# An encoder layer on eight cores: smaller bias table, reordered loads and stores, work moved between VectorE, GpSimd and ScalarE

**Chip, cores, metric.** One Trainium2 chip, all 8 cores, each with its own share of the tokens. The metric is the device time of the slowest core in microseconds (us). A program on all cores has a second, slower state in some of its executions: the four cores of one die, or of both, show a lower granted TensorE clock (0.82 to 0.96 in the slow runs of the changed kernel, 0.98 in its fast ones) and the run takes longer (4537 to 5164 us instead of 4422 to 4430). "Fast" below means a run without that. Four runs of the kernel before were there at the start, with a median of 4583.62 us (4518.32 to 4875.31); two of the four were fast.

## The reference, cut to what matters

```python
h = rmsnorm(x); q, k, v, u = split(h @ w_in)       # D = 2048, 16 heads of 64, 1024 pooling channels
attn = longnet(q, k, v)     # three dilated windows (128,1), (512,4), (2048,16), ALiBi penalty
pool = per group of 256 channels: mean over 2/4/8/16 tokens minus the token, a linear map, a scale
x = x + concat(attn, pool) @ w_out
x = x + relu(rmsnorm(x) @ w1) ** 2 @ w2            # DFF = 8192
y = rmsnorm_final(x)
```

## The kernel before

A scheduler records every operation with the tiles it reads and writes and derives the waits. Each core goes through these stages: K and V of ten half blocks of 512 tokens; the pooling channels of three units of 1024 tokens, with Q; attention in 24 steps; then for each of three units the output projection and the FFN. K, V, h and the attention result go through HBM. "SP" is the queue that issues plain transfers; weights, f32 in HBM and bf16 in their tiles, come through GpSimd's queue (the FFN's in loads of 2048 KB, a median of 14.9 us each in the kernel before). An evacuation is the copy of a finished group of matmuls out of PSUM, where TensorE leaves it (L419: 128x512 in a median of 681 ns). A run is a stretch of contiguous bytes in HBM that a transfer reads. A queue stands while it waits for a semaphore before it can issue its next transfer (from 421 to 452 us SP's stood 16.27 and 13.33 us). `acts` is the result of attention and pooling, x the input of the layer, X the residual that the output projection adds to.

The four places the argument touches, cut (cuts marked `# ...`):

```python
def prep(i):                       # half i of x becomes hT (scaled) and c0 (sum of squares)
    for q in range(4):             # x comes in four quarters of 1 MB
        # ... 4 scalings on VectorE (L366); Square on ScalarE
        if q > 0:
            S.pool(... c0.ap = c0.ap + b.ap ...)          # 2048 wide, L376
            if i + 1 < NHS: load_x(4 * i + q + 4)
    # ... two halving adds on VectorE (L384, L386)

# in first_k(i), i < 2:
for _ in prep(i + 1): pass         # the whole preparation of the next half ...
if i == 0: load_wv()
for m in (6, 7): k_group_mms(...); k_evac(i, m, b)        # ... ahead of two K evacuations (L419)

# in the V loop of half i, group gi:
win0 = window_copy("L0", 6, (0, 5), 2)                    # HBM to HBM, 2 copies of 2 MB
if i == 5 and gi % 4 == 2: next(win0)

# last attention step, and the FFN's first weights:
if si == NSTEP - 1 and it == 0:
    load_acts(UORD[0])             # both halves of the attention result, runs of 1 KB
    load_wo(0)
    for q in range(4): load_res(UORD[0], 0, q)            # residual X
# ... load_wo(1), load_wo(2), load_wo(3) straight behind
for m in range(16):
    oproj(1, m)
    # ...
    if m == 3: load_w1(0)          # 2 MB
```

The softmax here doesn't subtract the row's maximum and nothing guards it: scores larger than these inputs give would overflow.

## Time and profile before

Stages are read from the first and last start of four kinds of instruction on every core: the V evacuations, the exponentials of attention, the relus of the FFN and the last operation on y. The mean of the eight cores of the profiled (fast) run:

| stage | from, to | us |
|---|---|---|
| start | 0 to first V evacuation | 197.2 |
| K/V loop | to last V evacuation | 471.6 |
| pooling and Q | to first exponential | 222.0 |
| attention | to last exponential | 476.8 |
| entry to the FFN | to first relu | 160.3 |
| FFN, with two changes of unit | to last relu | 2881.2 |
| end | to last operation on y | 92.3 |
| sum | | 4501.4 |

Spans of the cores run from 4487.7 to 4524.1 us. The lines behind each stage stand in the prediction; in a timeline line the bracket at the end is the idle time before the group and what ended it.

### The profile page before, as it was taken

The numbers are of one execution on the slowest core, as the hardware profiler recorded it, in microseconds if no ns is written. First come the engines' busy times: TensorE is split into PE (matmuls) and PEld (weight loads), VectorE is DVE, ScalarE is ACT, GpSimd is POOL, SyncE is SP. The second block draws the span as 40 slices with busy tenths as digits, with TensorE's granted clock in tenths as the row PEclk, the third lists the DMA queues.
The fourth block names the chain that finished last, engine by engine and source line by source line (L and its number), as shares of the span: only waits on it lengthen the run. The fifth ranks groups of instructions, "written<-read, shape, count | busy, mean of one in ns | idle before, by whom it ended". The sixth has DMA issues, their size and how long they took to land.

```text
span 4524.1 us, 62014 instructions; the slowest of 8 cores (4487.7 to 4524.1 us)
## 1 busy us (share of the span) xinstructions
PE 4265.9 (94%) x23228; PEld 2085.8 (46%) x23228; DVE 2248.8 (50%) x3383; ACT 905.0 (20%) x1218; POOL 507.2 (11%) x381
## 2 busy tenths in 40 slices
PE   6799999799995999999999899999999899999996
PEld 2344445377773444444444344444444344444442
DVE  2224427866661344455556344444446445444446
ACT  1122210087782100000002100000002100000002
POOL 2122212300001200000005200000004200000003
PEclk8899999899998999999999999999999899999998
DMA  7376758499997533333355623333345623333332
GB/s 177 107 208 175 212 127 198 121 254 255 247 250 192 93 75 75 75 75 75 75 112 148 149 60 79 80 80 77 75 85 148 158 57 75 77 80 79 79 77 75
DMA packets 187077, 556.11 MB, mean 123 GB/s; under 512 B 14658, under 2 KB 118210, under 8 KB 158402
## 3 DMA queue, kind: packets, MB, share of 16 engines
q0 software_dynamic: 19536, 249.05, 28.2%
q1 hardware_dynamic: 167250, 303.09, 23.4%
q8 instruction: 194, 3.18, 0.3%
q14 instruction: 97, 0.79, 0.1%
HBM read 715.13 MB, written 105.91 MB: 181 GB/s over the span
## 4 chain that ended last, share of the span: by engine, by line
PE 80%; DMA 8%; DVE 5%; POOL 2%; issue 2%; SPq 1%; another core or an unknown queue 1%; ACT 1%; DVEq 0%; POOLq 0%; ACTq 0%
PE ps L296 80%; DMA y<-arena 3%; POOL arena L1048 1%; DVE arena L643 1%; SPq L140 1%; DMA arena<-wk 1%; POOL arena L376 1%; DVE arena L657 1%; DVE arena L1062 1%; DMA VD<-VD 1%; DVE arena L366 1%; DMA arena<-HT 1%; DMA arena<-xkv 1%; DMA arena<-xres 0%
## 5 line engine op out<-in xcount | busy, mean ns | idle before, releaser
L296 PE MATMUL ps<-arena 128*128 128x512 bf16 (+4 forms) x23228 | 4265.9, 347 | 238.0 <-DMA arena<-ACTD 42.9
L296 PEld LDWEIGHTS ps<-arena 128*128 128x128 bf16 x23228 | 2085.8, 102 | 2416.5 <-issue 319.0
L1097 DVE TENSOR_TENSOR arena<-ps,arena 128x512 f32<-128x512 f32 x1536 | 1052.6, 691 | 241.7 <-PE ps L296 239.7
L1087 DVE TENSOR_TENSOR arena<-arena 128x512 bf16<-128x512 f32 x384 | 265.3, 692 | 1056.9 <-ACT arena L1086 1056.9
L1086 ACT ACTIVATE arena<-ps 128x512 f32<-128x512 f32 x384 | 229.3, 597 | 2255.7 <-PE ps L296 2255.7
L140 POOL DMA_DIRECT2D arena<-w x96 | 51.0, 534 | 2362.1 <-PE ps L296 2361.3
L881 ACT ACTIVATE arena<-ps 128x1024 bf16<-128x1024 f32 x288 | 282.4, 1020 | 106.8 <-PE ps L296 87.2
L1048 POOL TENSOR_TENSOR arena<-arena 128x512 f32<-128x512 f32 x180 | 239.2, 1329 | 361.3 <-ACT arena L1047 348.5
L897 DVE TENSOR_TENSOR arena<-arena 128x1024 bf16<-128x1024 bf16 (+2 forms) x384 | 205.4, 556 | 94.4 <-ACT arena L881 86.7
L1073 DVE TENSOR_TENSOR arena<-ps,arena 128x512 f32<-128x512 f32 x96 | 65.6, 686 | 264.6 <-DMA arena<-xres 153.1
L1047 ACT ACTIVATE arena<-arena 128x512 f32<-128x512 f32 x180 | 113.2, 630 | 337.7 <-DVE arena L1073 276.6
L366 DVE TENSOR_SCALAR arena<-arena 128x512 bf16<-128x512 f32 x160 | 113.3, 762 | 132.0 <-DMA arena<-xkv 111.8
L376 POOL TENSOR_TENSOR arena<-arena 128x2048 f32<-128x2048 f32 x27 | 123.2, 4561 | 464.7 <-ACT arena L371 464.1
L419 DVE TENSOR_TENSOR arena<-ps,arena 128x512 bf16<-128x512 f32 x80 | 53.2, 684 | 103.4 <-PE ps L296 98.3
L447 ACT ACTIVATE arena<-ps,arena 128x512 bf16<-128x512 f32 x80 | 53.5, 687 | 252.2 <-PE ps L296 121.0
L371 ACT ACTIVATE arena<-arena 128x2048 f32<-128x2048 f32 x40 | 75.7, 1906 | 138.4 <-DVE arena L366 138.2
L944 DVE TENSOR_TENSOR arena<-ps,arena 64x512 bf16<-64x512 f32 x96 | 62.0, 684 | 77.2 <-ACT arena L938 77.2
L1062 DVE SCALAR_TENSOR_TENSOR arena<-arena 128x512 f32<-128x512 f32 x96 | 90.7, 987 | 3.4 <-ACT arena L325 3.4
L1057 DVE SCALAR_TENSOR_TENSOR arena<-arena 128x512 bf16<-128x512 f32 x96 | 74.1, 816 | 4.8 <-ACT arena L325 4.8
L631 POOL TENSOR_TENSOR arena<-arena 128x1039 f32<-128x1039 f32 x24 | 60.0, 2500 | 135.3 <-DVE arena L795 117.9
L140 POOL DMA_DIRECT2D arena<-wo x12 | 6.4, 539 | 581.1 <-PE ps L296 581.1
L322 DVE TENSOR_SCALAR arena<-ps 128x512 f32<-128x512 f32 (+1 forms) x23 | 15.3, 667 | 112.5 <-PE ps L296 112.5
(38 smaller groups left out, 471.3 us busy)
## 6 DMA issues: line engine op xcount, KB each, us to landing
arena<-w POOLq DMA_DIRECT2D x96, 2048.0 KB, 14.9
arena<-xkv SPq DMA_DIRECT2D x40, 1024.0 KB, 7.9
arena<-VD SPq DMA_DIRECT2D x72, 512.0 KB, 9.7
VD<-arena SPq DMA_DIRECT2D x48, 512.0 KB, 8.7
arena<-wo POOLq DMA_DIRECT2D x12, 2048.0 KB, 23.5
arena<-xres SPq DMA_DIRECT2D x24, 1024.0 KB, 7.1
y<-arena SPq DMA_DIRECT2D x96, 256.0 KB, 6.6
arena<-KT SPq DMA_DIRECT2D x144, 128.0 KB, 4.0
```

Of the source, the lines that this page charges most:

```text
L140: return self.op(eng, lambda e: e.dma_start(out=out() if callable(out) else out, in_=in_() if callable(in_) else in_), reads, writes, key=key)
L296: S.pe(lambda e: e.matmul(out, lhsT=lhsT, rhs=rhs, start=start, stop=stop, skip_group_check=skip), reads, writes)
L366: S.dve(lambda e, b=b, k=k, kc=kc: e.tensor_scalar(out=t[:, kc, :], in0=b[:, k, :], scalar1=cst[:, G1 + kc:G1 + kc + 1], scalar2=None, op0 ...
L376: S.pool(lambda e, b=b: e.tensor_tensor(out=c0.ap, in0=c0.ap, in1=b.ap, op=ALU.add), [c0.r(), b.r()], [c0.r()])
L881: S.act(lambda e: e.activation(out=e_.ap, in_=ps[:, 512 * sb:512 * sb + 1024], func=AF.Exp, scale=0.125), [P(sb), P(sb + 1)], [e_.r()])
L897: S.dve(lambda e, ov=ov, iv=iv, tv=tv: e.tensor_tensor(out=ov, in0=iv, in1=tv, op=ALU.mult), [e_.r((c0, c0 + n)), tb.r(hl)], [p_.r((c0, c0 ...
L1047: S.act(lambda e: e.activation(out=s_.ap, in_=x[:, m, :], func=AF.Square), [x.r(m)], [s_.r()])
L1048: S.pool(lambda e: e.tensor_tensor(out=acc[h].ap, in0=acc[h].ap, in1=s_.ap, op=ALU.add), [acc[h].r(), s_.r()], [acc[h].r(), ("serial",)])
L1062: S.dve(lambda e: e.scalar_tensor_tensor(out=X[h][:, m, :], in0=X[h][:, m, :], scalar=cst[:, GF + m:GF + m + 1], in1=rb3[h].ap, op0=ALU.mu ...
L1086: S.act(lambda e: e.activation(out=r_.ap, in_=ps8[:, b, :], func=AF.Relu), [P(b)], [r_.r()])
L1087: S.dve(lambda e: e.tensor_tensor(out=a_[:, fc, 512 * h:512 * h + 512], in0=r_.ap, in1=r_.ap, op=ALU.mult), [r_.r()], [a_.r(fc, (512 * h, ...
L1097: S.dve(lambda e: e.tensor_tensor(out=X[h][:, m, :], in0=ps8[:, b, :], in1=X[h][:, m, :], op=ALU.add), [P(b), X[h].r(m)], [X[h].r(m)])
```

## The change

Its intent is to close the places where TensorE waits: at the start, at the window copy, in the pooling stage, at the entry to the FFN, and at each change of unit; and to shrink the bias table so that one multiply does the work of two. Cut to its core:

```diff
-TABW = 1280
+TABW = 768                                   # one 256-wide table per pattern; masked blocks by strided PSUM columns
-y  [3, 2, 16, 128, 512]   ACTD [3, 2, 16, 128, 512]
+y  [3, 2, 128, 16, 512]   ACTD [3, 2, 128, 16, 512]      # 16 KB runs; y stored in pairs
 # prep: halving adds 1024, 512, 512, on GpSimd for q < 3, on VectorE for q = 3
+            op = S.pool if q < 3 else S.dve
 # first_k: only half of the next preparation ahead of the evacuations
-            for _ in prep(i + 1): pass
+        for _ in range(4): next(gn, None)
         if i == 0: load_wv()
         for m in (6, 7): ...
+        for _ in gn: pass
 # window copy: four copies of 1 MB in halves 4 to 7
-    win0 = window_copy("L0", 6, (0, 5), 2)
+    win0 = window_copy("L0", 6, (0, 5), 4)
-            if i == 5 and gi % 4 == 2:
+            if 4 <= i <= 7 and gi == 2:
 # pooling: the first add moves from GpSimd to VectorE, with a multiply; PSUM evacuation to ScalarE
-        S.pool(... s1 = uu + uu shifted ...)
+        S.dve(... uu = uu * rb ...)
+        S.dve(... s1 = uu + uu shifted ...)
 # entry to the FFN
+            if si == 18 and it == 2: load_acts(UORD[0], 0)
             if si == NSTEP - 1 and it == 0:
-                load_acts(UORD[0])
                 load_wo(0)
+                load_acts(UORD[0], 1)
 # ... load_wo(1..3) wait for X; the first evacuations lag by up to five groups
 # change of unit
-            pop_tail(2)
+            pop_tail(4 if m < 3 else 2)           # stores of y leave earlier
 # ... residual loads are asked for behind later stores
```

## The prediction

> **What bounds the kernel now.** I read the cores first: spans of 4487.7 to 4524.1 us, the two dies within 0.1%, so the profiled run is undisturbed. The four timed runs are 4518.32, 4519.07, 4648.17 and 4875.31 us; the last two are the slow state, and I predict against 4518.7, the fast pair. Then the table by stretches, which shows what a busy stage looks like:
>
> ```profile
> 1695.00:1808.00 113.00, 113.00 (x525) 51.18 (x524) 55.29 (x81) 10.16 (x17) 2.11 (x4) 1.00 0.36 75
> 904.00:1017.00 113.00, 111.76 (x1399) 87.90 (x1397) 75.67 (x129) 92.35 (x99) 0.00 (x0) 1.00 1.01 255
> ```
>
> The first is the FFN: TensorE has no gap, 525 matmuls in 113 us. In the long FFN stretch 3962 matmuls take 858 us, 0.2166 us each. It is over half of the span and the diff does not touch it. The second is attention: TensorE again has no real gap, but DMA is at 1.01, so nothing may be added there. What can be won lies where TensorE waits; I listed its timeline and kept the lines with a gap in brackets:
>
> ```profile
> 87.26 31.05 PE L296 MATMUL ps<-arena 128*128 128x512 bf16 x133 [20.20 <-DVE arena L419]
> 124.50 2.29 PE L296 MATMUL ps<-arena 128*128 128x512 bf16 x5 [6.19 <-DVE arena L366]
> 146.80 28.52 PE L296 MATMUL ps<-arena 128*128 128x512 bf16 x120 [20.01 <-DVE arena L419]
> 1417.79 22.42 PE L296 MATMUL ps<-arena 128*128 128x512 bf16 x90 [42.86 <-DMA arena<-ACTD]
> 2554.70 0.59 PE L296 MATMUL ps<-arena 128*128 128x512 bf16 x1 [11.10 <-DVE arena L1057]
> ```
>
> Two gaps of 20 us at the start wait for the K evacuation (L419); one of 43 us waits for the attention result read back from HBM; one of 11 us is at a change of unit. What holds L419 back stands in the timelines of GpSimd and VectorE:
>
> ```profile
> 69.61 14.37 POOL L376 TENSOR_TENSOR arena<-arena 128x2048 f32<-128x2048 f32 x3 [63.63 <-ACT arena L371]
> ...
> 84.49 1.22 DVE L384 TENSOR_TENSOR arena<-arena 128x1024 f32<-128x1024 f32 x1 [14.15 <-POOL arena L376]
> 85.82 0.69 DVE L386 TENSOR_TENSOR arena<-arena 128x512 f32<-128x512 f32 x1
> 86.43 1.28 DVE L419 TENSOR_TENSOR arena<-ps,arena 128x512 bf16<-128x512 f32 x2
> ```
>
> [...] the sum of squares of the next half waits 14 us for three GpSimd adds of 4.5 us, and the two evacuations that free PSUM banks stand behind it. The pooling stage (695 to 897 us) is bound by VectorE:
>
> ```profile
> 706.70 5.43 DVE L643 TENSOR_TENSOR arena<-arena 128x1037 f32<-128x1037 f32 x3
> ...
> 743.35 1.70 DVE L651 TENSOR_TENSOR arena<-arena 128x16 f32<-128x16 f32 x1
> ...
> 764.12 3.86 DVE L657 SCALAR_TENSOR_TENSOR arena<-arena 128x256 bf16<-128x256 f32 x4 [0.18 <-DVE arena L651]
> ```
>
> Three adds should be 3 x 1.23, a 16-element multiply is 0.17 elsewhere, four L657 are 2.14 elsewhere. Each chunk has one operation that is about 1.6 us too long, while GpSimd runs L631. Last, the change of unit, as the chain of work has it:
>
> ```profile
> 2505.13 41.42 DMA y<-arena
> 2546.78 6.33 DMA arena<-xres
> ```
>
> The last residual load waits for four output stores that took 41 us, against 6.5 for the group before them; VectorE stood 24.12 us for that load and TensorE 11 behind it.
>
> [...] L643 is 1.23 or 2.76 us, and L366 between 0.47 and 4.75. [...] a 2 MB weight load was issued from GpSimd at 2502.94, the four stores at 2503.14. [...] Here the first six matmuls after the gap of 42.86 took 2.72 us, 0.45 each.
>
> **The change, part by part.**
>
> *Start.* The sum of squares is cut into halving adds (1024, 512, 512 wide), GpSimd takes three quarters and VectorE the fourth, and the two evacuations now stand after the first eight of sixteen scalings instead of after the whole preparation. The evacuations then run at 67 instead of 86.4, so the first gap falls from 20.2 to under 1. GpSimd's chain is as long as before (estimate 13 to 14 us, from 1.3 us per 512 and 1.9 to 2.3 per 1024), but starts one quarter earlier and nothing but the sum waits on it. The second gap goes likewise, but there the next 1 MB of x (13.3 us to land in this trace) becomes the limit: it is asked for near 90 instead of 110.5, while 4 MB of Wv, which moved to about 77, and three x quarters are in flight. At the 180 GB/s of 90 to 120 us in this trace, 8 MB from 77 are through by 118 (estimate), so I let it land at 113 instead of 123.9. That is 10 us on that wait plus 19 of the second gap. Sum: 29 us at 146.8, not 40.
>
> *Window copy.* Two copies of 2 MB in one half become four of 1 MB in four halves. Before, the queue stood 16.27 + 13.33 us at 421 to 452, x came late and 52 matmuls, 11 us, were missing in 452 to 565. I give it 8, as each small copy still waits for the last V store.
>
> *Pooling stage.* The add L631 moves from GpSimd to VectorE, the PSUM evacuation (2 x 0.75) to ScalarE (2 x 0.6, idle there), and VectorE gets one 1024-wide multiply. Per chunk on VectorE: minus 1.51, minus about 1.6 of blocking, plus 1.23 and 1.24: minus 0.6. Per unit of eight chunks the old rates are 2 x (9.52 + 8.2 + 6.85 + 6.2) = 61.5; new 2 x (8.97 + 7.74 + 6.5 + 5.28) = 57.0, against TensorE's 8 x 6.93 = 55.4. Three units: 13.5; I take 12, since the 8.2 us wait for an ACTD store stays.
>
> *Attention.* Two multiplies (556 + 285 ns) become one (692): 96 x 0.149 = 14 us of VectorE, which is 67% busy there and not on the path: 0. The table falls from 640 to 384 KB, 6% of a step's estimated 4.3 MB; the gaps near the loads of HT (about 15 us in all over two places) shrink a little, but a 2 MB load of acts enters at step 18 of 24. The matmuls have the same number and width, with strided PSUM columns. Net 2.
>
> *Into the FFN.* The first half of acts is loaded five steps early, in 16 KB runs instead of 1 KB; the second half, the first weights and X follow in the last step, later weights behind X, and the first evacuations lag five banks. TensorE can start near 1376, if the first weight tile (issued at 1355.5, 15 us alone, sharing with 6 MB) has landed. About 18 MB remain to be moved; at 300 to 380 GB/s, which the large packets reached from 1418 to 1448, that ends near 1420 to 1430, about as TensorE consumes them. I take 37 of 42.9, with 6 left as small stalls.
>
> *Change of unit, twice.* Stores become 512 KB pairs, residual loads are asked for after later stores, so the queue need not stand, and the tail is popped twice as fast in the first three steps, so all stores are out before the FFN weights come. From the matmul counts the first change loses 31 us ((1048 - 904) x 0.2166, from 2373 to 2600), the second 36. What stays: 6.46 us for the GpSimd square chain before the first row norm, about 2 for the second norm, which is now asked for earlier than GpSimd finishes, and about 2.5 of restart. So 20 + 25 = 45.
>
> *End.* Same chain, last store twice as big: 0 to minus 1.
>
> Sum: 29 + 8 + 12 + 2 + 37 + 45 = 133; 4518.7 - 133 is 4386; I say 4390.
>
> **The rivals.** First, DMA takes the place of the waits removed: the start and the entry to the FFN were both at a DMA share of 1.0 while TensorE stood (1.00 from 1376 to 1418). If bytes are all that counts, they give 10 and 20 instead of 29 and 37, and the time is 4426. For it: the share. Against: 165 to 177 GB/s there, against 384 later at the same share[...]. Second, attention pays: with a share of 1.01 the early acts load or strided PSUM writes stop a step; 1% of slower matmuls costs 5 us, a doubled HT gap 10: 4400. Third, VectorE becomes the bound in preparation, blocked by nine short GpSimd adds instead of three long ones, and K evacuations come late in all ten halves: 1 to 2 us each, 4405. Fourth, all gaps close: 20 + 20 + 43 + 60 + 12 + 11 = 166, 4353.
>
> **Range and chances.** The first two together make about 4435, the fourth 4353. Eight times in ten the time lies in 4350 to 4455; the upper end also holds a median that a slow run has touched. Two per cent is 90 us: it needs a third of my sum to fail. Faster by over 2%: 0.87; within: 0.12; slower: 0.01.
>
> **What will show it.** Gaps before the matmuls near 68 and 114 us: under 1, and about 17. No VectorE wait of 14 us for GpSimd at 84. No L643, L651 or L657 beyond 1.3, 0.2 and 0.6 us each, and the pooling stage some 190 instead of 202 us. Attention steps at 19.2 us. The first matmul of the output projection within 7 us of attention's last. VectorE's waits for xres (153.1 us in all before) mostly gone, and no y store of 40 us; the 6.46 us gaps stay. I am wrong if the attention step grows, if the weights of the output projection arrive one by one after TensorE wants them, or if K evacuations wait for the new adds.

## The result, and the profile after

The changed kernel took a median of 4483.37 us over 10 runs (4422.13 to 5163.88), the kernel before 4594.09 over 15 runs beside it (4516.2 to 5119.31). Half of the 10 runs were slow, and so were 8 of the 15. The five fast runs lie between 4422.13 and 4430.09, the seven fast ones of before between 4516.2 and 4523.0. Ratios here are the mean time of one kernel's fast runs over that of the other's fast runs of the same rounds, so not quite the ratio of the medians: 0.9793, 95% interval 0.978 to 0.9806. The fast time fell by 94 us; the prediction had 129.

By stage, mean of eight cores, with the prediction's term beside it:

| stage | before | after | gained | predicted |
|---|---|---|---|---|
| start | 197.2 | 177.0 | 20.2 | 29 |
| K/V loop | 471.6 | 469.6 | 2.0 | 8 |
| pooling and Q | 222.0 | 216.5 | 5.5 | 12 |
| attention and entry | 637.1 | 605.5 | 31.6 | 2 + 37 |
| FFN, two changes of unit | 2881.2 | 2846.9 | 34.3 | 45 |
| end | 92.3 | 92.1 | 0.2 | 0 |
| sum | 4501.4 | 4407.6 | 93.8 | 133 |

Every term but the last came out smaller. The predicted terms were read on core 5, the slowest of the kernel before. From there to core 2, the slowest of the changed kernel, the gains are 19.3, 2.1, 7.6, 27.4, 42.9 and 0.4, in all 99.7: the changes of unit are nearly as predicted on that core. Taken apart, attention went from 476.8 to 475.8 and the entry from 160.3 to 129.8. TensorE's timeline of the changed kernel, its groups behind a gap of interest:

```profile
67.47 19.80 PE L296 MATMUL ps<-arena 128*128 128x512 bf16 x89 [0.87 <-DVE arena L416]
...
124.00 1.91 PE L296 MATMUL ps<-arena 128*128 128x512 bf16 x4 [26.97 <-DVE arena L366]
...
613.55 230.00 PE L296 MATMUL ps<-arena 128*128 128x512 bf16 x1219 [8.78 <-ACT arena L444]
...
1347.69 15.01 PE L296 MATMUL ps<-arena 128*128 128x512 bf16 x62 [1.65 <-DMA arena<-wo]
1375.16 104.00 PE L296 MATMUL ps<-arena 128*128 128x512 bf16 x457 [12.46 <-DMA arena<-wo]
...
2489.32 872.59 PE L296 MATMUL ps<-arena 128*128 128x512 bf16 x3958 [0.71 <-DVE arena L1057]
```

The first 20 us gap is down to 0.87, the 43 us gap at the entry to 1.65 and 12.46, the 11 us gap at the change of unit to 0.71. But the second gap at the start grew from 20 to 27, and there is a new one of 8.78 us at 613. The chain of work names what these two waited for:

```profile
89.22 33.66 DMA arena<-xkv
...
580.69 31.94 DMA VD<-arena
```

A quarter of x (1 MB) took 34 us to land, where it had taken 13 in the kernel before; a V store (512 KB) took 32. Both times weights had been issued from GpSimd's queue shortly before (at 580.07 the second time, 0.6 us ahead of the store), here at the start:

```profile
76.38 4.47 POOL L140 DMA_DIRECT2D arena<-wv x8
```

And VectorE's timeline, at the K evacuation (L416) and in the pooling stage:

```profile
66.64 1.28 DVE L416 TENSOR_TENSOR arena<-ps,arena 128x512 bf16<-128x512 f32 x2
...
696.65 3.91 DVE L645 TENSOR_TENSOR arena<-arena 128x1037 f32<-128x1037 f32 x3
...
731.09 2.12 DVE L659 SCALAR_TENSOR_TENSOR arena<-arena 128x256 bf16<-128x256 f32 x4 [9.02 <-DMA ACTD<-arena]
...
746.23 1.23 DVE L631 TENSOR_TENSOR arena<-arena 128x1024 f32<-128x1024 f32 x1 [1.97 <-ACT arena L797]
```

The evacuations run at 66.64 as predicted. The three adds that took 5.43 us take 3.91. New are waits of 1.97 us for ScalarE's evacuation, three on each core. The wait for a store of the pooling result is 9.02 us here and 9.3 to 14.2 on the other cores (mean 11.5); before it was 7.9 to 10.1 (mean 8.9).

In attention and at the entry the columns of the table by stretches are: stretch, its length, busy time and count of PE, PEld, DVE, ACT and POOL, granted clock, DMA share, GB/s:

```profile
904.00:1017.00 113.00, 110.65 (x1376) 87.89 (x1399) 74.47 (x106) 92.64 (x99) 0.00 (x0) 1.00 0.94 247
...
1350.00:1375.00 25.00, 12.64 (x58) 5.49 (x56) 0.00 (x0) 0.00 (x0) 1.59 (x3) 0.84 1.03 230
```

The DMA share is near 1 from 900 to 1400 (0.92 to 1.02 in stretches of 100 us on core 2), while TensorE is busy and while it waits.

### The profile page after: what moved, and what is told of

It reads as the page before. It is cut to its first block, busy times and chain, and to the rows that moved or that the text cites.

```text
span 4424.4 us, 61370 instructions; the slowest of 8 cores (4403.6 to 4424.4 us)
## 1 busy us (share of the span) xinstructions
PE 4226.2 (96%) x22791; PEld 2081.9 (47%) x23228; DVE 2252.3 (51%) x3296; ACT 938.6 (21%) x1266; POOL 450.7 (10%) x402
## 3 DMA queue, kind: packets, MB, share of 16 engines
q1 hardware_dynamic: 148850, 296.79, 23.3%
## 4 chain that ended last, share of the span: by engine, by line
PE 78%; DMA 8%; DVE 6%; POOL 3%; SPq 2%; issue 2%; ACT 1%; DVEq 0%; POOLq 0%; ACTq 0%
PE ps L296 78%; SPq L140 2%; DMA VD<-arena 2%; POOL arena L1048 2%; DMA arena<-xkv 2%; DVE arena L366 1%; DMA arena<-wk 1%; DMA VD<-VD 1%; DMA arena<-wo 1%; DVE arena L659 1%; DVE arena L645 1%; DVE arena L1062 1%; DVE arena L633 1%; DVE arena L631 1%; DVE arena L416 0%
## 5 line engine op out<-in xcount | busy, mean ns | idle before, releaser
L896 DVE TENSOR_TENSOR arena<-arena 128x1024 bf16<-128x1024 bf16 x288 | 198.8, 692 | 99.5 <-ACT arena L885 98.3
L366 DVE TENSOR_SCALAR arena<-arena 128x512 bf16<-128x512 f32 x160 | 127.6, 851 | 150.6 <-DMA arena<-xkv 130.5
L416 DVE TENSOR_TENSOR arena<-ps,arena 128x512 bf16<-128x512 f32 x80 | 53.3, 685 | 111.6 <-PE ps L296 106.6
L374 POOL TENSOR_TENSOR arena<-arena 128x1024 f32<-128x1024 f32 x27 | 64.2, 2379 | 429.8 <-ACT arena L402 255.5
L659 DVE SCALAR_TENSOR_TENSOR arena<-arena 128x256 bf16<-128x256 f32 x96 | 51.3, 604 | 13.1 <-DMA ACTD<-arena 9.0
## 6 DMA issues: line engine op xcount, KB each, us to landing
arena<-w POOLq DMA_DIRECT2D x96, 2048.0 KB, 13.8
```

The source lines that it names most:

```text
L366: S.dve(lambda e, b=b, k=k, kc=kc: e.tensor_scalar(out=t[:, kc, :], in0=b[:, k, :], scalar1=cst[:, G1 + kc:G1 + kc + 1], scalar2=None, op0 ...
L659: S.dve(lambda e, i0=i0, i1=i1, oo=oo: e.scalar_tensor_tensor(out=oo, in0=i0, scalar=1.0 / w, in1=i1, op0=ALU.mult, op1=ALU.subtract), [cu ...
L896: S.dve(lambda e: e.tensor_tensor(out=p_.ap.rearrange("p (a b) -> p a b", b=256), in0=e_.ap.rearrange("p (a b) -> p a b", b=256), in1=tv, ...
```

## The experiments

Eighteen kernels ran, all with the right result; seventeen are edits of the changed kernel and one (e6) of the kernel before. Unless said otherwise a figure is the mean of the eight cores of a fast profiled run, and each edit of the changed kernel is compared with the 177.0, 469.6, 216.5 and 605.5 us of the table. Each is one profiled run, and the cores of one run differ: in the changed kernel four cores have 464 us in the K/V loop and four 473 to 478, and pooling is 214 or 219. The runs differ as well. In the undisturbed profiles whose edit leaves a stage alone, its mean is 174.1 to 177.0 us at the start, 464.3 to 469.6 in the K/V loop, 215.2 to 219.2 in pooling and 601.9 to 605.6 in attention and entry. The changed kernel's own profile stands at the upper end of three of these, so a gain measured from it can be up to 5 us too large, and a loss as much too small; differences under 5 us need a wait in the trace to back them.

### The start: weights of V beside x

**e1**: the loads of Wv moved behind the requests for x, by making them wait for a tile of x.

```diff
-... wv_d[:, 2 * k:2 * k + 2, :], [],
+... wv_d[:, 2 * k:2 * k + 2, :], [xs[0].r()],      # and issued in the next half
```

> The changed kernel, but the eight Wv loads wait until the first quarter of x for the third half has landed. Theory: that quarter, asked for at 89 us, took 34 us to land only because it shares the DMA engines with Wv. Then it lands in 10 to 15 us, the gap of 27 us before the third half's matmuls at 124 falls to 7 to 12, Wv still lands before the first V matmul, and attention starts 15 to 20 us earlier (its first exponential at about 850 instead of 867). Rival 1, bytes are all that counts: the gap falls, but the first V half then waits for Wv, and attention starts at 862 to 868. Rival 2, the quarter is behind the three other quarters of x in its own queue: it still takes over 25 us and nothing moves.

The quarter of x landed near 101 and the gap of 27 us fell to 5.59. But the start stayed at 177.2: a new gap of 22.75 stood at 149. The loads of Wv had become readers of the x buffer, and its next writer, ScalarE's square, waited for them. That is an artifact of the edit; the total settles nothing, the gap does. **e1b** takes a wait without that side effect, on the first scaled column of the third half.

```diff
-... wv_d[:, 2 * k:2 * k + 2, :], [],
+... wv_d[:, 2 * k:2 * k + 2, :], [hT[2].r(0)],      # and issued in the next half, as in e1
```

> The first try at holding Wv back made the squares of the third half wait for Wv as well, because the loads were marked as readers of the x buffer that the squares overwrite; that closed nothing. Here the Wv loads wait for the first scaled column of the third half instead, which nothing overwrites soon. Theory: the first quarter of x lands in 10 to 15 us as in that run, the gap of 27 us falls to under 8, the third half's sum of squares is not late any more, and the first V evacuation comes at 155 to 165 us instead of 177. Rival: Wv (30 us of transfer from about 101) now is what the first V half waits for, and the first V evacuation comes at 170 or later.

The quarter of x landed in 12.6 us, the start took 153.7 us, 23.3 less, and the run 4400.07. TensorE's timeline, and GpSimd's:

```profile
101.54 2.29 PE L296 MATMUL ps<-arena 128*128 128x512 bf16 x5 [5.52 <-DVE arena L366]
```

```profile
101.94 4.99 POOL L140 DMA_DIRECT2D arena<-wv x8 [17.85 <-DVE arena L366]
```

With Wv issued at 102 instead of 76 the gap is 5.5 us. The change moved the evacuations off the path as planned; that it gained 20 us and not 43 is the collision of x with Wv (the quarter took 33.66 us to land beside Wv, 12.6 ahead of it).

### The K/V loop

**e3**: the weights for folding the pooling map (wuT, 4 loads) wait for the last V store of half 8.

```diff
-... wuT_d[:, 2 * k:2 * k + 2, :], [],
+... wuT_d[:, 2 * k:2 * k + 2, :], [("VD", HS[8][0], 4 * HS[8][1] + 3)],
```

> The changed kernel, but the four wuT loads (1 MB each) wait until the last V store of the ninth half (i=8) has landed. Theory: the stall of 8.8 us of TensorE at 613 us, which the kernel before does not have, comes from wuT being issued 0.6 us before four V stores that then take 32 us to land. Then the stores land in under 15 us, the stall is under 1 us, no new wait for wuT appears at the weight product near 640, and attention starts 7 to 10 us earlier. Rival: the stores come late because their mask fill on VectorE stands behind the preparation of the next half; then the stall stays over 5 us.

Two of its three runs were slow, and in the profiled one cores 2 and 3 ran at clock 0.973. On the six other cores the K/V loop took 464 to 466 us. Time from issue to landing of the V stores at 570 to 600 us, core 2 of the changed kernel:

```profile
DMA to landing us min/median/max: 31.8/31.9/32.1
```

Core 4 of e3, and its TensorE, which has no gap where core 2 had 8.78:

```profile
DMA to landing us min/median/max: 3.3/4.2/5.3
```

```profile
539.68 140.58 PE L296 MATMUL ps<-arena 128*128 128x512 bf16 x827
```

So the slow stores come from wuT beside them: a V store takes 26.7 us or more on every core of the changed kernel, and at most 9.1 on the six cores of e3. But the stores stop TensorE on three cores of the changed kernel only (0, 2 and 6, by 8.3, 8.8 and 11.1 us), and in e4b (below), which leaves this part as it is, on none. The gain is that of some cores. The pooling stage took 220.3, 3.8 more; 2.3 of that is a longer wait for the pooling store, and that mean is near the scatter, so no cost of the later weights is shown.

**e11** put the bias table back to its old size, the extra 256 KB a step loaded but unused. It was meant for attention (below), and showed something else too.

```diff
-TABW = 768
+TABW = 1280           # the columns beyond 768 stay zero
```

> The changed kernel with only the bias table back at its old size (640 KB a step instead of 384, the extra 256 KB unused). The sum of the two stages from the first to the last attention exp and from there to the first relu was 605.5 us (mean of 8 cores) in the changed kernel and 637.1 in the kernel before. Theory A (these stages are set by what the DMA engines have to move; share 0.98 to 1.04 from 900 to 1400): 24 x 256 KB is 6.3 MB, at some 250 GB/s 25 us, so the sum grows by 15 to 25 us. Theory B (my prediction: TensorE sets the attention step, the table hardly matters): plus 0 to 5.

The K/V loop rose from 469.6 to 490.8 on all cores: the table is cast from HBM to HBM in this loop, 640 KB a half instead of 384. SP's queue and VectorE show how 256 KB cost that much. SP:

```profile
336.62 0.75 SPq L140 DMA_DIRECT2D VD<-arena x1
353.06 0.68 SPq L140 DMA_DIRECT2D VD<-VD x1
```

VectorE:

```profile
495.44 0.88 DVE L366 TENSOR_SCALAR arena<-arena 128x512 bf16<-128x512 f32 x2 [24.55 <-DMA arena<-xkv]
```

The queue stands 15.7 us between a V store and the window copy, because the copy waits for the V store just issued; x, asked for behind it, comes late. In the changed kernel the same stand is there (460.83 to 475.64), but x comes just in time: four cores have 464 us. **e15** keeps the old table and puts the copy ahead of this half's V stores:

```diff
-            if 4 <= i <= 7 and gi == 2:
+            if 4 <= i <= 7 and gi == 0:      # with TABW = 1280
```

> The changed kernel with the old table size (as e11) and the four small window copies put behind the first V group of a half instead of the third, so before this half's V stores instead of just behind one. With the old table the K/V loop took 488 to 494 us on the 8 cores; TensorE alone needs 464. Theory A (the queue stands 15 us for the V stores ahead of each copy, x is asked for late, and the larger table then makes it late enough to stop TensorE): the queue's stand before each copy falls under 3 us and the K/V loop to 464 to 474. Theory B (the bytes of the larger table as such): 485 or more.

```profile
338.18 4.55 SPq L140 DMA_DIRECT2D HT<-arena x1
343.24 0.98 SPq L140 DMA_DIRECT2D VD<-VD x1
```

The stand is 0.5 us, and the K/V loop 474.2, just above the range of theory A: three cores at 464, and five at 478 to 481, which are the cores with the wuT stall (8.9 to 12.6 us at 612 to 617). So the standing queue made 16.7 of the 21 us. Splitting the window copy hid it in the changed kernel because the smaller table made room.

### Pooling

**e9** puts the first add back on GpSimd.

```diff
-        S.dve(lambda e: e.tensor_tensor(out=s1[:, 1:1040], ...
+        S.pool(lambda e: e.tensor_tensor(out=s1[:, 1:1040], ...
```

> The changed kernel with the first pooling add back on GpSimd. Theory A ([...] each such add stretches one VectorE operation by about 1.6 us, more than the 1.23 that VectorE saves): one of L643/L651/L653/L659 per chunk beyond its usual length again, the pooling stage of 216.5 us (mean of 8 cores) plus 3 to 10. Theory B (the blocked VectorE time wasn't what bound the stage): within 2 or shorter.

Its runs were slow; in the profiled one cores 4 to 7 were, and on the undisturbed die (cores 0 to 3) pooling took 222.3, 219.7, 223.9 and 221.1 us against 213.6 to 214.4 there in the changed kernel, 7.8 more in the mean. The size is less sure than the sign: the same four cores have 214.0 to 220.6 in twelve runs that leave pooling alone, and 2.1 of the 7.8 are a longer wait for the store. Chunk by chunk on core 2 e9 takes 0.1 to 0.4 us longer, about 5 us in 24 chunks. GpSimd, then VectorE:

```profile
694.24 2.79 POOL L633 TENSOR_TENSOR arena<-arena 128x1039 f32<-128x1039 f32 x1 [6.22 <-DVE arena L631]
```

```profile
694.00 5.45 DVE L645 TENSOR_TENSOR arena<-arena 128x1037 f32<-128x1037 f32 x3
```

Three adds take 5.45 us beside the GpSimd add and 3.91 without: 1.54 us lost, as the prediction read it; VectorE gets most of that back, as it has the add no longer.

**e2** lets the pooling buffers go round by a running count of chunks instead of the chunk number modulo 3, which reuses a buffer too soon where a unit changes.

```diff
-        uu = ub[m % 3]
+        uu = ub[cidx(u, m) % 3]        # cidx = 8 * u + 7 - m; the same for ap_
```

> The changed kernel, with the three pooling buffers taken in turn by a chunk counter instead of by m modulo 3 (the same for the three output tiles). Theory: at the two changes of unit the old numbering gives m=7 the buffer of m=1, two chunks back, so that ScalarE's evacuation starts only when VectorE is done, and VectorE then waits 1.97 us for it, four times; with the counter these waits of VectorE for ScalarE go, and the pooling stage (first ScalarE evacuation to first attention exponential, 193 us) is 4 to 8 us shorter. Rival: the stage is bound elsewhere (TensorE at 6.93 us a chunk, or the 9 us wait for an ACTD store), and the stage shrinks by less than 2.

The waits of 1.97 us are gone (three on each core, not the four that were expected), and the stage is 213.3, 3.2 less, between the theory and its rival. The wait for the store stays (14.0 us on core 2, 7.5 on core 5), and six cores have a second one of 2.2 to 3.4 us. The run, 4431.13, shows nothing of it, since cores 2 and 3 ran at clock 0.978. **e10** makes the other two window copies, which pass in this stage, one transfer each instead of two.

```diff
-window_copy("L2", 8, (0, 2), 2)      window_copy("R1", 7, (3, 5), 2)
+window_copy("L2", 8, (0, 2), 1)      window_copy("R1", 7, (3, 5), 1)
```

> The changed kernel, with each of the two window copies of the pooling stage made as one DMA of 4 MB instead of two of 2 MB, of which the second waits for the first in the queue with the stores of the pooled tiles behind it. Theory: VectorE's wait of 9 to 14 us for an ACTD store at about 722 to 731 us falls to under 3 us, and the pooling stage (last V evacuation to first exponential, 217 us in the mean over the cores) is 6 to 10 us shorter. Rival: the store is slow because the copy fills the DMA engines; then the wait stays over 6 us.

215.1 us, and the wait for the store 4.6 to 13.8, over 6 on six of the cores: the rival, and within the scatter.

### Attention and the entry to the FFN

Back to **e11**: attention and entry rose from 605.5 to 617.1, 11.6 us for the table alone; theory A had 15 to 25, the prediction next to nothing. e15, with the same old table, has 616.3. Three runs undo one part of the entry each. **e12** takes the old layout of the attention result (1 KB runs), **e13** loads its first half in the last step and not at step 18, **e5** frees the second weight load from waiting for X.

```diff
 # e12
-ACTD [3, 2, 128, 16, 512]
+ACTD [3, 2, 16, 128, 512]
 # e13
-            if si == 18 and it == 2: load_acts(UORD[0], 0)
+                load_acts(UORD[0], 0)          # in the last step, with the other half
 # e5
-                load_wo(1, [X[0].r((0, 4))])
+                load_wo(1)
```

> The changed kernel with only the layout of the attention result in HBM as before (runs of 1 KB instead of 16 KB in the three 2 x 2 MB reads). Theory A (DMA time of small runs is what the entry to the FFN had lost; the prediction put most of its 37 us on it): the sum of attention and entry, 605.5, grows by 8 us or more, and the two loads take over 25 us each. Theory B (only the order of the loads and the lag of the evacuations matter): plus 0 to 4.

> The changed kernel with the first half of the attention result loaded with the second in the last attention step, not at step 18. Theory A (the stages from 900 to 1400 are bound by the DMA engines as a whole, so it doesn't matter where the 2 MB are moved): the sum 605.5 stays within 4 us, attention gets 8 to 10 shorter, the entry that much longer. Theory B (the early load is what hides the entry, as predicted): attention 3 to 6 shorter, the entry over 12 longer, sum plus 8 or more.

> The changed kernel, but the second weight tile of the output projection does not wait for the first quarter of X. Theory: it is issued at about 1331 instead of 1352.5 and lands 10 us or more before the 1375 of the changed kernel; the gap of 12.5 us falls to under 5, the time from the last attention exponential to the first relu falls from 125 to 136 us by 6 to 10. Rival: DMA is at its limit from 1326 to 1406 whatever the order; then the first weight tile, the evacuations or the later tiles come late by as much, and that time stays within 3 us.

The sums are 605.3, 604.5 and 604.6: nothing, three times. In e13 attention is 10.3 shorter and the entry 9.2 longer, as theory A had it. In e5 four cores have 484 to 491 us in attention and 117.5 in the entry, the other four 466 to 472 and 132 to 137: the wait moves, the sum stays. Taken alone, this would say that the layout and the early load are worth nothing. They replace each other, as **e16** and **e17** show. e16 takes the order of the kernel before, with 16 KB runs; e17 that order with 1 KB runs.

```diff
 # e16
-            if si == 18 and it == 2: load_acts(UORD[0], 0)
-                load_wo(0)
-                load_acts(UORD[0], 1)
+                load_acts(UORD[0], 0)
+                load_acts(UORD[0], 1)
+                load_wo(0)                     # load_wo(1..3) without waiting for X
 # e17: the same, and ACTD as in e12
```

> The changed kernel (small table, 16 KB runs, lagged evacuations) with the loads of the entry to the FFN in the order of the kernel before: both halves of the attention result first and in the last step, then the first weights and X; no weight load waits for X. Attention plus entry was 605.5 (mean of 8 cores). Theory A (order: four weight loads of 2 MB side by side with the result and X delay what TensorE needs first): plus 10 to 20. Theory B (all bytes must pass anyway): within 4.

> As e16 and the attention result in runs of 1 KB as before; what then still differs from the entry of the kernel before are the table and the lag of the evacuations. Theory A (order and layout make the remaining 20 us together): 620 to 628. Theory B (order alone): as e16 within 3. Theory C (the lag): under 612.

e17 has 625.8 us, and the old gap is back. TensorE, then SP's queue:

```profile
1377.56 116.51 PE L296 MATMUL ps<-arena 128*128 128x512 bf16 x518 [42.02 <-DMA arena<-ACTD]
```

```profile
1317.58 49.32 SPq L140 DMA_DIRECT2D arena<-ACTD x2
1367.04 12.06 SPq L140 DMA_DIRECT2D arena<-xres x4
```

e16 has 597.2, better than the changed kernel by 8, which neither theory had. TensorE, then SP's queue:

```profile
1347.82 29.77 PE L296 MATMUL ps<-arena 128*128 128x512 bf16 x125 [8.12 <-DMA arena<-ACTD]
1383.47 88.56 PE L296 MATMUL ps<-arena 128*128 128x512 bf16 x393 [5.88 <-DVE arena L1079]
```

```profile
1322.73 0.92 SPq L140 DMA_DIRECT2D arena<-ACTD x2
```

Issuing the two loads took 49.32 us in 1 KB runs (48.8 of them for the second) and 0.92 in 16 KB runs, and they landed after a median of 62.5 us against 33.7, beside the same weight loads. X could be asked for only at 1367. The books close: from 637.1 to e17's 625.8 is 11.3 (table and lag of the evacuations; e11 gave 11.6 for the table), from there to e16's 597.2 is 28.6 (layout, in the old order), and the new order gives 8.3 of it back.

Why it gives back is seen in SP's queue. In the changed kernel:

```profile
1232.49 0.33 SPq L140 DMA_DIRECT2D arena<-ACTD x1
1251.02 0.38 SPq L140 DMA_DIRECT2D ACTD<-arena x1
```

The early load of 2 MB has to land before the next attention result is stored, 18 us in which the queue stands and the V loads of the next step come late. TensorE stops for them:

```profile
1256.55 9.76 PE L296 MATMUL ps<-arena 128*128 128x128 bf16 x86 [4.31 <-DMA arena<-VD]
```

The rule behind it is the scheduler's: a transfer that reuses a semaphore waits for all who waited on it. **e4** cut the early load into seven pieces over steps 16 to 22, **e4b** gave the stores of each unit a semaphore of their own.

```diff
 # e4
-            if si == 18 and it == 2: load_acts(UORD[0], 0)
+            if 16 <= si <= 22 and it == 2: ... two (at the last four) of 16 rows, semaphore "acts0" ...
 # e4b
-..., "ast%d" % (si % 2))
+..., "ast%d%d" % (u, si % 2))
```

> The changed kernel, but the first half of acts (2 MB) is loaded in seven pieces over attention steps 16 to 22 instead of at once in step 18. Theory: DMA is full in attention, and the single load is what stops steps 19 and 20 for about 9 us (at 1243 to 1279); in pieces it fits into what the smaller table freed, and attention takes 469 to 472 us instead of 478. Rival: there is no room at all, the 2 MB cost the same wherever they are, and attention stays at 476 to 479 with several small gaps.

> The changed kernel, where the stores of the attention result use one semaphore per unit and parity instead of one per parity. In the changed kernel the next such store after the early load of acts shares a semaphore that this load waited on, so the scheduler makes the store wait until the load has landed (18.5 us in the queue), and the V loads behind it come late. Theory: that is the stop at 1243 to 1279, not the 2 MB; then the store follows within 10 us, the gaps before V there are under 2 us together, and attention takes 6 to 10 us less (sum of attention and entry to the FFN, over the cores 605 us in the mean: 596 to 600). Rival: the bytes; then the store goes early but the V loads still land late and the sum stays at 603 or more.

e4 failed: attention took 501.9 us, 26 more, as the queue now stood 8 to 9 us behind each piece. e4b has 598.1, 7.4 less (3.8 below the lowest of the runs that leave these stages alone), TensorE waits for no V between 1195 and 1300 us on the four cores looked at (0, 1, 2 and 5), and the store follows the load at once:

```profile
1225.29 1.13 SPq L140 DMA_DIRECT2D arena<-ACTD x1
1226.52 0.38 SPq L140 DMA_DIRECT2D ACTD<-arena x1
```

### The change of unit

**e6** edits the kernel before in one number: the first 2 MB weight load of the FFN comes three groups later.

```diff
-            if m == 3: load_w1(0)
+            if m == 6: load_w1(0)
```

> The kernel before with only the first weight load of the FFN asked for three output groups later (m = 6 instead of 3). Theory A (the 41 us of the four output stores at each change of unit come from the 2 MB weight load beside them, as the prediction read it): the stores at about 2505 take under 15 us, VectorE's wait of 24 us for the residual load and TensorE's gap of 11 us at 2554 go, and the time falls by 10 to 20 us. Theory B (the stores are slow of themselves, by size or number): stores still over 30 us, the gap stays.

All three runs were slow; in the profiled one cores 0 to 3 were (clock 0.94), and cores 4 to 7 ran undisturbed. There the FFN stage took 2845.2 to 2847.3 us, where the same cores had 2871.1 to 2889.6 (mean 2880.9): 34.5 us, the whole gain of the change in this stage, and more than the 10 to 20 of theory A. Time from issue to landing of the eight output stores at 2470 to 2490, core 7, kernel before:

```profile
DMA to landing us min/median/max: 6.7/11.8/26.3
```

and e6:

```profile
DMA to landing us min/median/max: 6.3/6.5/7.1
```

TensorE on core 7, in the kernel before:

```profile
2533.06 0.59 PE L296 MATMUL ps<-arena 128*128 128x512 bf16 x1 [9.10 <-DVE arena L1057]
```

and in e6:

```profile
2390.90 128.17 PE L296 MATMUL ps<-arena 128*128 128x512 f32 x577 [6.46 <-POOL arena L1048]
2519.78 872.58 PE L296 MATMUL ps<-arena 128*128 128x512 bf16 x4039 [0.70 <-DVE arena L1057]
```

The stores were slow because of the weight load beside them (26.3 us at most beside it, 7.1 ahead of it). Larger stores, faster draining and later residual loads were not needed for these 34 us.

### All together

**e18** joins e1b, e2, e3, e4b, e10 and the earlier window copies of e15 on the changed kernel (with the small table); **e19** adds e16's order of loads.

> All mended together on the changed kernel: Wv loads behind the first scaling of the third half (23 us in e1b), pooling buffers by a running count (3), last pooling weights behind the V stores (0 to 5), separate semaphores of the attention result's stores by unit (7), window copies of the middle two slots in one piece each (1) and the first slot's copies before the V stores (0 to 6). Sum 34 to 45: the slowest core at 4380 to 4392 against 4424, faster than the kernel before by 2.8 to 3.1%. Rival: the stages hand each other's gain on (as attention and entry did), and no more than e1b's 4400 comes out.

> e18 with the entry to the FFN loaded in the old order (16 KB runs and small table kept). e16 had 597.2 us for attention and entry where the changed kernel had 605.5 and e18 600.6. Theory A (all weights may be in flight early once the result comes in 16 KB runs): 3 to 8 us below e18's 4386 to 4393, so 4379 to 4388. Theory B (e16's gain was the removed queue stand, which e18 has already): within 3 of e18.

e18 had two fast runs of four, 4386.28 and 4392.57. Its stages: 153.5, 463.8 (on every core), 214.5, 600.6, 2846.5, 92.4; the sum is 36.3 us below the changed kernel's, within the 34 to 45 expected. In the K/V loop TensorE has nothing left to win:

```profile
200.00:650.00 450.00, 449.73 (x2269) 214.62 (x2268) 181.78 (x305) 110.83 (x135) 88.14 (x63) 1.00 0.68 185
```

e19 had four fast runs, 4383.94, 4384.2, 4387.76 and 4417.98 (in the last, cores 2 and 3 ran at clock 0.978), against a median of the fast runs of before of 4516.35. The ratio of fast runs is 0.9731, interval 0.9695 to 0.9766. Attention and entry took 596.4 against e18's 600.6, and the sum of the stages is 2.3 us below e18's, as theory B had it. The old order gives 4.2 us in that stage here and gave 8.3 in e16, so about half of e16's advantage may have been the queue that e4b had already freed; differences of that size are near the scatter. e19's interval lies below that of the changed kernel (0.978 to 0.9806), and e18's two fast runs 30 us below the changed kernel's fastest.

## Why the prediction was right or wrong

**The steps that failed.** The waits that the prediction named were there and closed nearly as it said. Its range did not hold a median of which half of the runs were slow. In the sum, 133 us became 93.8, and two steps failed in their mechanism: at the start it let x land beside Wv ten microseconds too soon, and in attention it gave no worth to the bytes that the smaller table saves. In the window copy, in pooling and at the entry the waits were right and the terms mis-sized: what stood behind the wait that closed was not added up.

**The number.** 4390 with a range of 4350 to 4455 was meant for the fast state; the fast runs, 4422 to 4430, lie in the range, the median of all runs, 4483, does not. Half of the runs were slow, and a range whose "upper end also holds a median that a slow run has touched" held no such median. The four runs of before, two of them slow, had warned of this. Apart from that, the middle was 35 us too low, and the chance of 0.87 for over 2% too high: the fast ratio is just about 2%.

**Start.** Right: the evacuations at 67 and the first gap under 1. The term that failed is the landing of x, "so I let it land at 113": it landed at 123, because 4 MB of Wv were loaded beside it (33.66 us, against 12.6 in e1b). The prediction named this collision and undersized it, and its own figures say so: 8 MB from 77 at 180 GB/s take 44 to 47 us and end at 121 to 124, not "by 118". That is 10 us of the sum, and by e1b 23 us were to be had.

**Window copy.** 8 predicted, 2.0 measured. "Each small copy still waits for the last V store" was right and is the reason (e15); the term was mis-sized, and new stalls of 8.3 to 11.1 us from wuT beside the V stores (e3), on three of the cores, were not foreseen. With the scatter of this stage the gain can be up to 7.

**Pooling.** That GpSimd's add holds VectorE up was right (e9: three adds take 5.45 us beside it, 3.91 without; 7.8 us of the stage); by what mechanism is not shown. 12 became 5.5; what the trace has in its place are waits that the term left out: the buffer rotation (three of 1.97 us, 3.2 by e2) and a store that is waited for 2.6 us longer than before in the mean. Why that store is slower stays open; e10 tried one cause.

**Attention.** Here the step failed, not only its size. "DMA is at 1.01, so nothing may be added there" was read, and its reverse was not drawn: in this stage, bytes taken out were gain. The stage went from 476.8 to 475.8, close to the "Net 2", but by luck: the smaller table is worth 13.3 us in it (e11 has 489.1), and the early load of acts takes 10.3 back (e13 has 465.5). Over attention and entry the table is worth 11.6 and, with the queue as it stands, 21 in the K/V loop, where the prediction did not count it.

**Into the FFN.** 37 predicted; the entry alone fell by 30.5, but 9.2 of that is the early load, which attention pays for (e13). Attention and entry together gave 31.6, of which the table made about 11.6, so 20. The prediction listed four causes (layout, earlier load, order, lag) and gave none a size of its own. In the old order the layout alone gives 28.6; the new order costs 8.3 of that.

**Change of unit.** The cause, stores beside the weight load, was right (e6, core 7: 7.1 us at most ahead of it, 26.3 beside it in the kernel before); by what mechanism is not shown. 45 was read on the slowest core, whose FFN stage did fall by 42.9 to the 2846.7 of the changed kernel's slowest core; the mean of the cores lost 34.3. What the prediction did not see is that moving the weight load is enough.

**The rivals.** The first, DMA in place of the waits, was the nearest: at the start and at the entry TensorE's remaining gaps end with x (26.97 us) and with weights (1.65 and 12.46 us). Its 4426 is the mean of the fast runs, but by luck: it had 10 us at the start, where 20 came, and the other terms fell short too. The second came in its first half: the early load of acts stops a step (4.31 us on core 2) and costs attention 10 us, which the smaller table hides. The strided PSUM writes cost nothing that shows: undisturbed groups of TensorE take 19.05 to 19.07 us after and 19.06 to 19.08 before. The third, late evacuations in all ten halves, did not come: four cores run the K/V loop in 464 us.

**Open.** Why 6.3 MB less table (24 steps of 256 KB) gives 11.6 us, where the 247 GB/s measured from 904 to 1017 would give some 25, and what the lag of the evacuations gives by itself, was not tested. Nor is it known why cores whose V stores are as slow as those of cores 0, 2 and 6 do not stop for them.

## What to carry to other kernels

Where a transfer is slow, list what it shares its time with: moving one weight load by three groups gave what a rewrite of the stores gave (34.5 us in e6, 34.3 in the change). Undo parts of a change in pairs as well as singly; two parts that each look worthless may be replacing each other. A wait that seems harmless can delay what the queue is asked for behind it, and it shows only when the slack is used up: SP's queue stood some 15 us before a window copy both in the changed kernel, where four cores ran the K/V loop in 464 us all the same, and in e11, where it made 16.7 us of the 21. Profile the unchanged parts too: what a stage does in runs that leave it alone is the scatter against which a gain is read.
